# Rows and constants on GpSimd's queue, first weights issued by ScalarE, other banks for one projection, units dealt out anew

## The chip, the cores and the metric

The kernel runs on one core of one Trainium2 chip. TensorE (PE) multiplies, PEld is its loading of weights; VectorE (DVE), ScalarE (ACT) and GpSimd (POOL) work on tiles in the on-chip memory, and SyncE (SP) here only issues transfers. Each engine runs its own instructions in a fixed order and waits on semaphores for the others. The metric is the time of the whole program on the device in microseconds, as a median of several executions.

## The reference

One decoder layer for 256 tokens of width 2048, in fp32: a combined projection, two kinds of attention, their gated merge, an MLP with squared ReLU, and a gated embedding.

```python
h = rmsnorm(x, g_mix)
proj = h @ w_in                                  # 2048 -> 10240
qa, ka, va, qb, kb, vb, ga, gb = jnp.split(proj, splits, axis=-1)
ya = dilated_mixture(qa, ka, va)                 # three windowed patterns, 8 heads
yb = stick_breaking(qb, kb, vb)                  # 8 heads
merged = sigmoid(ga) * (ya @ w_branch_a) + sigmoid(gb) * (yb @ w_branch_b)
x = x + merged @ w_out
x = x + jnp.square(jax.nn.relu(rmsnorm(x, g_mlp) @ w_up)) @ w_down   # D_FF = 8192
x = x + (p @ w_ple_proj) * sigmoid(rmsnorm(x, g_ple) @ w_ple_gate)
```

## The kernel before

Every fp32 operand is split into two parts of a faster format: ScalarE copies it to a rounded high part (`wh` for weights, L82; with a gain for `h`, L85), and VectorE subtracts that from the original to get the low part (`wl`, L83; L86). A product is then three matmuls, high·high, high·low and low·high (L137 to L139 in the projections). Weights come in tiles of 1 MB by `load` on SP's queue (L91) into `raw`; `raw`, `wh` and `wl` have three buffers each, so a transfer, a split and a matmul of different tiles overlap and each waits for the buffer that it takes.

**Start.** The first projection runs in groups of 512 output columns; a group takes four chunks of weights, four 128-row pieces of the 2048 each. The first group has a function of its own, `first_weights(c)` for c = 0 to 3: it loads the columns of transposed x (`load_x`, L183) and the chunk of weights (L192 in three parts for c = 0, L91 after it), splits four pieces of `h` out of `x0` or `x1`, and splits the weights. With c = 3 it also calls `load_rows` (L229), which brings x by rows as `xr0` and `xr1`, 1 MB each, and loads the identity `idt`, the constants `cs` and the gains `gq` (L201 to L203). `xr0` and `xr1` lie in the pool of `x0` and `x1` and take over their buffers, so these loads wait until `x0` and `x1` have been read. ScalarE squares the rows (L232) for the norm `rt` (L212 to L219), which scales the projection's results (L250).

**MLP.** The hidden width is done in eight stages of 1024. `up_units(s)` makes a stage's 16 half units: per 128 hidden columns 16 pairs of matmuls, one of 512 columns (L526) and one of 256 (L527), then `ev` and the sum `hs` (L533), and `hidden` (L502 to L511) with ScalarE's square, four subtractions `hr` and the split into `u`. The way down has two halves of 1024 output columns per stage. In stages 0 to 6 the first half is done by `fast_units`: seven products in place of eight (L546, L548, L550, banks of the tag "s"), with sums of the weights' quarters `quart` on VectorE (L560, 128x2048) between them and sums of the products into the rows `xr` (L560 also, and `add_rows`, L446 and L448). The second half is done by `plain_units`, eight units (L628 to L630, two banks of the tag "m").

**The order.** `together` deals the units of three streams by due times: unit i of n of a stream with offset `first` is due at (i + first) / n. `up_units(s + 1)` runs in the same stage as the ways down of s. The program text that this makes is then ordered by a scheduler for each engine, and small works are put off by `later` until a modelled clock has advanced. The lines of the changed kernel are two less than those of before, from `first_weights` on.

Of the kernel before, what the change touches and what calls it, by code (L numbers as in the profile page):

```python
# [9 lines left out]
F32 = mybir.dt.float32  # L10
# [6 lines left out]
P = 128  # L17
# [5 lines left out]
DH = 128  # L23
# [6 lines left out]
C_ID, C_ONES, C_TRI, C_LOGC, C_SBM, C_COS, C_SIN = 0, 128, 256, 384, 768, 1152, 1184  # L30
# [29 lines left out]
def layer_kernel(ctx: ExitStack, tc: tile.TileContext, xt, xm, pt, gains, qkg, cst,  # L60
                 wa, wba, wbb, wo, wup, wdn, wpg, wpp, out):
    nc = tc.nc
# [26 lines left out]
    def load(src, nk, cols):  # L89
        raw = wts.tile([P, nk, cols], F32, tag="raw", name="raw")  # L90
        nc.sync.dma_start(raw.rearrange("p k c -> p (k c)"), src)  # L91
        return raw
# [89 lines left out]
    def load_x(a, b):  # L182
        nc.sync.dma_start(x[a // 8][:, a % 8:(b - 1) % 8 + 1, :], xt[:, a:b, :])  # L183

    def first_weights(c):

        k = 4 * c
        if c == 0:
            raw = wts.tile([P, 4, 512], F32, tag="raw", name="raw")
            for a, b in ((0, 1), (1, 2), (2, 4)):  # L190
                load_x(a, b)
                nc.sync.dma_start(raw[:, a:b, :].rearrange("p k c -> p (k c)"),  # L192
                                  wa[0, 0, :, a * 512:b * 512])
        else:
            load_x(k, k + 4)
            raw = load(wa[0, c], 4, 512)
        for i in range(k, k + 4):
            split(h[i][:, 0, :], h[i][:, 1, :], xs(i), gn[:, 0, i:i + 1])
        if c == 3:
            load_rows()  # L200
            nc.sync.dma_start(idt, cst[:, C_ID:C_ID + P])  # L201
            nc.sync.dma_start(cs, cst)
            nc.sync.dma_start(gq, bass.AP(tensor=qkg.tensor, offset=qkg.offset,  # L203
                                          ap=[[0, P], [DH, 2], [1, DH]]))
        return split_weights(raw, 4, 512, 1 if c == 0 else 2)

    def rows_norm(ss, name, pool):
# [17 lines left out]
    def load_rows():  # L225

        xr.extend(block([P, D], F32, f"xr{tt}", blk) for tt in range(2))
        for tt in range(2):
            nc.sync.dma_start(xr[tt], xm[tt])  # L229

    def squares_rows(tt, g, ss, junk):
        nc.scalar.activation(junk, xr[tt][:, g * PIECE:(g + 1) * PIECE], AF.Square,  # L232
# [259 lines left out]
    def bank2(tag, bufs=1):  # L492
        return ps2.tile([P, 512], F32, tag=tag, name=f"ps_{tag}", bufs=bufs)
# [21 lines left out]

    A21, A11, A22, A12, S3, S1, S2, S4 = range(8)

    def up_units(s, out, tag="mm"):

        for g in range(4):  # L520
            sums = mw.tile([P, 2, T], F32, tag="hs", name="hs", bufs=2)
            for j in range(2):
                ps = bank2(tag, 4 if tag == "s" else 2)
                parts = split_weights(load(wup[4 * s + g, j], DT, P), DT, P)
                for kt, (wh, wl) in enumerate(parts):
                    nc.tensor.matmul(ps, wh, flat(h2[kt]), start=kt == 0, stop=False)  # L526
                    nc.tensor.matmul(ps[:, :T], wl, h2[kt][:, 0, :], start=False, stop=kt == DT - 1)  # L527
                    advance(0.347)
                    if kt == 7:
                        yield  # L530
                t = mw.tile([P, T], F32, tag="ev", name="ev", bufs=2)
                nc.scalar.activation(t, ps[:, T:], AF.Copy)
                nc.vector.tensor_tensor(sums[:, j, :], ps[:, :T], t, op=ALU.add)  # L533
                if j == 1:
                    out.append(hidden(sums, (s, 0) in FAST or (s, 1) in FAST))
                yield
# [81 lines left out]
    def plain_units(s, n, u):  # L618

        for j in range(2):  # L620
            ps = [bank2("s", 4) if j and s == 7 else bank2("m", 2) for _ in range(2)]
            for i in range(2):
                raw = load(wdn[s, n, i, j], 4, PIECE)
                for k, (wh, wl) in enumerate(split_weights(raw, 4, PIECE)):
                    for tt in range(2):
                        a = 2 * i + tt
                        last = i == 1 and k == 3
                        nc.tensor.matmul(ps[tt], u[k][:, 0, a, :], wh, start=i + k == 0, stop=False)  # L628
                        nc.tensor.matmul(ps[tt], u[k][:, 0, a, :], wl, start=False, stop=False)  # L629
                        nc.tensor.matmul(ps[tt], u[k][:, 1, a, :], wh, start=False, stop=last)  # L630
                    advance(1.36)
                    if k == 1:
                        yield
                if i == 0:
                    yield
            for tt in range(2):
                add_rows(tt, (2 * n + j) * PIECE, ps[tt], r2[:, tt:tt + 1])
            yield
# [52 lines left out]
            finished(2 * n + 1)  # L691

    hids = [[]]
    for _ in up_units(0, hids[0], "s"):
        pass
    for s in range(7):
        hids.append([])
        streams = [(0.5, 16, up_units(s + 1, hids[s + 1]))]
        for n in range(2):
            if (s, n) in FAST:  # L700
                streams.append((0.3, 7, fast_units(s, n, hids[s])))
            else:
                streams.append((0.75, 8, plain_units(s, n, hids[s])))
        together(*streams)
    together((0.5, 16, last_units(hids[7])), (0.25, 4, embedding_units()))
    later(6, lambda: rms.append(rows_norm(ss2, "rt2", mw)))
# [88 lines left out]
```

## Time and profile before

| what | value |
|---|---|
| median of 3 runs | 1492.02 us (1491.55 to 1495.32) |
| profiled execution, own time | 1492.93 us |
| profiled execution, span of the trace | 1491.10 us |
| mean granted clock of TensorE | 0.997 of full |
| TensorE busy | 1470.8 us, 99% |
| VectorE busy | 1000.4 us, 67% |
| ScalarE busy | 840.3 us, 56% |
| GpSimd busy | 42.4 us, 3% |

All times of the trace are from one execution. Its own time is what the runs measure too; the span is the part that the trace covers, from its first instruction to its last. Matmuls overlap in the trace, so their spacing from start to start tells their cost, and the time printed for one does not.

### The profile page before, as it was taken

Reading aid. Unit: us, or ns where it says so; the run is one execution under the profiler, and the core shown is the slowest. Engines: PE = TensorE matmul, PEld = TensorE weight load, DVE = VectorE, ACT = ScalarE, POOL = GpSimd, SP = SyncE. Lnnn points to the kernel's source line nnn. Section 1 sums busy time; section 2 is a strip of 40 time slices with the busy share of each in tenths; the row PEclk is TensorE's granted clock in tenths of the full one; section 3 lists DMA queues with packets and bytes.
Section 4 is the critical chain, followed back from the end, with each engine's and each line's share of the span. In section 5 each row is a group of like instructions: output and inputs, shape, how many; then the busy total and the mean of one; then the engine's idle time right before and its main releaser. Section 6 shows DMA issues by size and latency. Waiting matters only on the chain.

```text
span 1491.1 us, 17831 instructions
## 1 busy us (share of the span) xinstructions
PE 1470.8 (99%) x6960; PEld 1210.2 (81%) x6960; DVE 1000.4 (67%) x1209; ACT 840.3 (56%) x1084; POOL 42.4 (3%) x60
## 2 busy tenths in 40 slices
PE   7999999999999999999999999999999999999998
PEld 5888888888888888888787887878888787878886
DVE  5775555456555555556878879788787878765654
ACT  7444555488834444546655656656565655656543
POOL 0442000000000000000000000000000000000000
PEclk9999999999999999999999999999999999999999
DMA  8555544544455555557455464645546465444563
GB/s 330 174 196 193 175 155 159 194 169 170 169 182 190 193 185 186 194 178 302 141 198 198 170 226 140 228 170 191 204 155 239 143 208 191 159 146 154 201 221 111
DMA packets 40549, 279.09 MB, mean 187 GB/s; under 512 B 4624, under 2 KB 5136, under 8 KB 7312
## 3 DMA queue, kind: packets, MB, share of 16 engines
q1 hardware_dynamic: 40320, 277.92, 53.5%
q8 instruction: 54, 0.88, 0.2%
q14 instruction: 31, 0.25, 0.0%
q10 hardware_dynamic: 144, 0.02, 0.0%
HBM read 275.83 MB, written 2.10 MB: 186 GB/s over the span
## 4 chain that ended last, share of the span: by engine, by line
PE 92%; DVE 3%; issue 2%; DMA 1%; ACT 1%; SPq 0%; DVEq 0%; ACTq 0%
PE ps_mm L137 13%; PE ps_mm L139 13%; PE ps_mm L526 13%; PE ps_mm L138 13%; PE ps_mm L527 7%; PE ps_m L629 4%; PE ps_m L630 4%; PE ps_m L628 3%; PE ps_s L548 3%; PE ps_s L546 2%; PE ps_s L550 2%; PE ps_s L526 2%; DVE wl L83 2%; DMA raw<-in_wa 1%; ACT wh L82 1%
## 5 line engine op out<-in xcount | busy, mean ns | idle before, releaser
L83 DVE TENSOR_TENSOR wl<-raw,wh 128x1024 fp32r<-128x1024 f32 (+1 forms) x462 | 563.5, 1228 | 341.3 <-ACT wh L82 337.8
L82 ACT ACTIVATE wh<-raw 128x1024 fp32r<-128x1024 f32 (+1 forms) x462 | 485.3, 1054 | 404.2 <-PE ps_mm L139 222.8
L526 PE MATMUL ps_mm<-h,wh 128*128 128x512 f32 x896 | 321.3, 398 | 0.0
L137 PE MATMUL ps_mm<-wh,h 128*128 128x512 f32 x640 | 255.8, 400 | 5.5 <-ACT wh L82 5.5
L527 PE MATMUL ps_mm<-h,wl 128*128 128x256 f32 x896 | 251.8, 281 | 0.4
L138 PE MATMUL ps_mm<-wl,h 128*128 128x512 f32 x640 | 251.2, 393 | 0.6 <-DVE wl L83 0.5
L139 PE MATMUL ps_mm<-wh,h 128*128 128x512 f32 x640 | 251.0, 392 | 0.0
L526 PEld LDWEIGHTS ps_mm<-h,wh 128*128 128x128 f32 x896 | 168.3, 188 | 40.8 <-ACT wh L82 2.3
L83 DVE TENSOR_TENSOR wl<-quart,wh 128x1024 fp32r<-128x1024 f32 x98 | 120.1, 1225 | 83.3 <-ACT wh L82 83.2
L527 PEld LDWEIGHTS ps_mm<-h,wl 128*128 128x128 f32 x896 | 169.0, 189 | 8.2 <-DVE wl L83 3.2
L82 ACT ACTIVATE wh<-quart 128x1024 fp32r<-128x1024 f32 x98 | 104.0, 1061 | 123.2 <-PE ps_mm L526 87.0
L137 PEld LDWEIGHTS ps_mm<-wh,h 128*128 128x128 f32 x640 | 121.0, 189 | 31.7 <-ACT wh L82 8.1
L138 PEld LDWEIGHTS ps_mm<-wl,h 128*128 128x128 f32 x640 | 121.3, 189 | 26.8 <-DVE wl L83 2.6
L139 PEld LDWEIGHTS ps_mm<-wh,h 128*128 128x128 f32 x640 | 121.0, 189 | 25.8
L629 PE MATMUL ps_m<-wl,u 128*128 128x512 f32 x256 | 101.8, 397 | 4.1 <-DVE wl L83 4.0
L630 PE MATMUL ps_m<-wh,u 128*128 128x512 f32 x256 | 100.0, 391 | 0.0
L628 PE MATMUL ps_m<-wh,u 128*128 128x512 f32 x256 | 97.9, 392 | 1.6 <-DVE xr L448 1.6
L548 PE MATMUL ps_s<-wl,u 128*128 128x512 f32 x196 | 80.2, 409 | 0.0
L546 PE MATMUL ps_s<-wh,u 128*128 128x512 f32 x196 | 78.6, 401 | 0.0
L550 PE MATMUL ps_s<-wh,u 128*128 128x512 f32 x196 | 76.7, 392 | 0.0
L560 DVE TENSOR_TENSOR quart<-quart 128x2048 f32<-128x2048 f32 x28 | 64.1, 2289 | 0.5
L629 PEld LDWEIGHTS ps_m<-wl,u 128*128 128x128 f32 x256 | 48.1, 188 | 18.1 <-DVE wl L83 9.2
(204 smaller groups left out, 1826.0 us busy)
## 6 DMA issues: line engine op xcount, KB each, us to landing
raw<-in_wa SPq DMA_DIRECT2D x79, 1024.0 KB, 4.8
raw<-in_wup SPq DMA_DIRECT2D x64, 1024.0 KB, 4.8
raw<-in_wdn SPq DMA_DIRECT2D x36, 1024.0 KB, 4.8
quart<-in_wdn SPq DMA_DIRECT2D x28, 1024.0 KB, 4.8
raw<-in_wo SPq DMA_DIRECT2D x16, 1024.0 KB, 4.8
raw<-in_wpg SPq DMA_DIRECT2D x16, 1024.0 KB, 4.8
raw<-in_wba SPq DMA_DIRECT2D x8, 1024.0 KB, 4.8
raw<-in_wbb SPq DMA_DIRECT2D x8, 1024.0 KB, 4.8
```

The costliest lines, as they stand in the source:

```text
L82: nc.scalar.activation(hi, src, AF.Copy)
L83: nc.vector.tensor_tensor(lo, src, hi.bitcast(F32), op=ALU.subtract)
L137: nc.tensor.matmul(ps[tt], lhs[kt][:, 0, t], wh, start=kt == 0, stop=False)
L138: nc.tensor.matmul(ps[tt], lhs[kt][:, 0, t], wl, start=False, stop=False)
L139: nc.tensor.matmul(ps[tt], lhs[kt][:, 1, t], wh, start=False, stop=kt == last)
L526: nc.tensor.matmul(ps, wh, flat(h2[kt]), start=kt == 0, stop=False)
L527: nc.tensor.matmul(ps[:, :T], wl, h2[kt][:, 0, :], start=False, stop=kt == DT - 1)
L546: nc.tensor.matmul(ps, f[k][:, 0, a, :], wh, start=start and k == 0, stop=False, skip_group_check=not start)
L548: nc.tensor.matmul(ps, f[k][:, 0, a, :], wl, start=False, stop=False, skip_group_check=not start)
L628: nc.tensor.matmul(ps[tt], u[k][:, 0, a, :], wh, start=i + k == 0, stop=False)
L629: nc.tensor.matmul(ps[tt], u[k][:, 0, a, :], wl, start=False, stop=False)
L630: nc.tensor.matmul(ps[tt], u[k][:, 1, a, :], wh, start=False, stop=last)
```

## The change

There are four edits. The rows of x and the three constants are issued by GpSimd, with `idt` ahead of the rows. The weights of the first group's chunks 0 and 1 are issued by ScalarE, those of chunks 2 and 3 by SP as before, and x comes by SP. The first up projection takes its banks from the tags "mm" and "m" in turn and no longer from "s". In `together` the fast units' offset goes from 0.3 to 0.6 and the plain units' from 0.75 to 0.3.

```diff
@@ -184,24 +184,22 @@
 
     def first_weights(c):
 
+
         k = 4 * c
-        if c == 0:
-            raw = wts.tile([P, 4, 512], F32, tag="raw", name="raw")
-            for a, b in ((0, 1), (1, 2), (2, 4)):
-                load_x(a, b)
-                nc.sync.dma_start(raw[:, a:b, :].rearrange("p k c -> p (k c)"),
-                                  wa[0, 0, :, a * 512:b * 512])
-        else:
-            load_x(k, k + 4)
-            raw = load(wa[0, c], 4, 512)
+        raw = wts.tile([P, 4, 512], F32, tag="raw", name="raw")
+        for a, b in ((0, 1), (1, 2), (2, 4)) if c == 0 else ((0, 4),):
+            load_x(k + a, k + b)
+            queue = nc.scalar if c < 2 else nc.sync
+            queue.dma_start(raw[:, a:b, :].rearrange("p k c -> p (k c)"),
+                            wa[0, c, :, a * 512:b * 512])
         for i in range(k, k + 4):
             split(h[i][:, 0, :], h[i][:, 1, :], xs(i), gn[:, 0, i:i + 1])
         if c == 3:
+            nc.gpsimd.dma_start(idt, cst[:, C_ID:C_ID + P])
             load_rows()
-            nc.sync.dma_start(idt, cst[:, C_ID:C_ID + P])
-            nc.sync.dma_start(cs, cst)
-            nc.sync.dma_start(gq, bass.AP(tensor=qkg.tensor, offset=qkg.offset,
-                                          ap=[[0, P], [DH, 2], [1, DH]]))
+            nc.gpsimd.dma_start(cs, cst)
+            nc.gpsimd.dma_start(gq, bass.AP(tensor=qkg.tensor, offset=qkg.offset,
+                                            ap=[[0, P], [DH, 2], [1, DH]]))
         return split_weights(raw, 4, 512, 1 if c == 0 else 2)
 
     def rows_norm(ss, name, pool):
@@ -226,7 +224,7 @@
 
         xr.extend(block([P, D], F32, f"xr{tt}", blk) for tt in range(2))
         for tt in range(2):
-            nc.sync.dma_start(xr[tt], xm[tt])
+            nc.gpsimd.dma_start(xr[tt], xm[tt])
 
     def squares_rows(tt, g, ss, junk):
         nc.scalar.activation(junk, xr[tt][:, g * PIECE:(g + 1) * PIECE], AF.Square,
@@ -515,12 +513,12 @@
 
     A21, A11, A22, A12, S3, S1, S2, S4 = range(8)
 
-    def up_units(s, out, tag="mm"):
+    def up_units(s, out, tags=("mm", "mm")):
 
         for g in range(4):
             sums = mw.tile([P, 2, T], F32, tag="hs", name="hs", bufs=2)
             for j in range(2):
-                ps = bank2(tag, 4 if tag == "s" else 2)
+                ps = bank2(tags[j], 2)
                 parts = split_weights(load(wup[4 * s + g, j], DT, P), DT, P)
                 for kt, (wh, wl) in enumerate(parts):
                     nc.tensor.matmul(ps, wh, flat(h2[kt]), start=kt == 0, stop=False)
@@ -691,16 +689,16 @@
             finished(2 * n + 1)
 
     hids = [[]]
-    for _ in up_units(0, hids[0], "s"):
+    for _ in up_units(0, hids[0], ("mm", "m")):
         pass
     for s in range(7):
         hids.append([])
         streams = [(0.5, 16, up_units(s + 1, hids[s + 1]))]
         for n in range(2):
             if (s, n) in FAST:
-                streams.append((0.3, 7, fast_units(s, n, hids[s])))
+                streams.append((0.6, 7, fast_units(s, n, hids[s])))
             else:
-                streams.append((0.75, 8, plain_units(s, n, hids[s])))
+                streams.append((0.3, 8, plain_units(s, n, hids[s])))
         together(*streams)
     together((0.5, 16, last_units(hids[7])), (0.25, 4, embedding_units()))
     later(6, lambda: rms.append(rows_norm(ss2, "rt2", mw)))
```

SP's queue behind the first group's last weights (`raw_237`), before. `raw_366` are the first weights of group 2:

```order
L91 DMA raw_237<-in_wa 128x2048
L229 DMA xr0_247<-in_xm 128x2048
L229 DMA xr1_248<-in_xm 128x2048
L201 DMA idt_84<-in_cst 128x128
L202 DMA cs_83<-in_cst 128x1216
L203 DMA gq_85<-in_qkg 128x256
L91 DMA raw_366<-in_wa 128x2048
```

And the whole start of SP's queue in the changed kernel, in which `raw_236` are the first group's last weights:

```order
L183 DMA x0_73<-in_xt 128x256 x2
L183 DMA x0_73<-in_xt 128x512
L183 DMA x0_73<-in_xt 128x1024
L193 DMA raw_193<-in_wa 128x2048
L183 DMA x1_74<-in_xt 128x1024 x2
L193 DMA raw_236<-in_wa 128x2048
L91 DMA raw_366<-in_wa 128x2048
```

The five transfers between the two have left SP's queue, and so have chunks 0 and 1 of the weights. GpSimd's queue in the changed kernel begins with these:

```order
L198 DMA idt_84<-in_cst 128x128
L200 DMA cs_83<-in_cst 128x1216
L201 DMA gq_85<-in_qkg 128x256
L227 DMA xr0_248<-in_xm 128x2048
L227 DMA xr1_249<-in_xm 128x2048
```

They are the only transfers of GpSimd, ahead of its other work. ScalarE's instructions at the start, before (`gn` are the gains, `raw_95` is chunk 0, `raw_151` chunk 1):

```order
L85 ACTIVATE h0_86<-x0_73,gn_75 128x256
L82 ACTIVATE wh_110<-raw_95 128x512
L85 ACTIVATE h0_86<-x0_73,gn_75 128x256
L82 ACTIVATE wh_114<-raw_95 128x512
L85 ACTIVATE h0_86<-x0_73,gn_75 128x256 x2
L82 ACTIVATE wh_118<-raw_95 128x512
L82 ACTIVATE wh_122<-raw_95 128x512
L85 ACTIVATE h1_87<-x0_73,gn_75 128x256 x4
L82 ACTIVATE wh_161<-raw_151 128x1024
```

And in the changed kernel, where chunk 1 is `raw_150`:

```order
L157 DMA gn_75<-in_gains 128x48
L193 DMA raw_95<-in_wa 128x512 x2
L193 DMA raw_95<-in_wa 128x1024
L85 ACT_TABLE_LOAD
L85 ACTIVATE h0_86<-x0_73,gn_75 128x256 x4
L82 ACTIVATE wh_110<-raw_95 128x512
L82 ACTIVATE wh_114<-raw_95 128x512
L82 ACTIVATE wh_118<-raw_95 128x512
L193 DMA raw_150<-in_wa 128x2048
L82 ACTIVATE wh_122<-raw_95 128x512
L85 ACTIVATE h1_87<-x0_73,gn_75 128x256 x4
L82 ACTIVATE wh_161<-raw_150 128x1024
```

The four splits of `h0` moved ahead of the first weights, and the issue of chunk 1 stands behind `wh_118`.

VectorE in a steady stage of the MLP, before. Names on `quart` are quarters of the fast units' weights, `raw` weights of the up projection or the plain units:

```order
L83 TENSOR_TENSOR wl_7035<-raw_7032,wh_7034 128x1024
L83 TENSOR_TENSOR wl_7039<-raw_7032,wh_7038 128x1024
L83 TENSOR_TENSOR u_6934<-hr_6928,u_6934 128x1024
L533 TENSOR_TENSOR hs_6951<-ps_mm_6952,ev_7027 128x256
L560 TENSOR_TENSOR quart_6981<-quart_6981,quart_6983 128x2048
L83 TENSOR_TENSOR wl_7058<-raw_7055,wh_7057 128x1024
L83 TENSOR_TENSOR wl_7062<-raw_7055,wh_7061 128x1024
L560 TENSOR_TENSOR xr1_248<-xr1_248,cp_7008 128x512
L83 TENSOR_TENSOR wl_7083<-quart_6979,wh_7082 128x1024
L83 TENSOR_TENSOR wl_7093<-quart_6979,wh_7092 128x1024
L560 TENSOR_TENSOR quart_6979<-quart_6979,quart_6983 128x2048
L83 TENSOR_TENSOR wl_7151<-raw_7148,wh_7150 128x1024
```

And at a like place in the changed kernel; `wl_7786` and `wl_7790` are up weights, `wl_7852` and `wl_7862` weights of a fast product, `wl_7878` the next up weights:

```order
L83 TENSOR_TENSOR wl_7751<-quart_7731,wh_7750 128x1024
L531 TENSOR_TENSOR hs_7679<-ps_mm_7680,ev_7779 128x256
L558 TENSOR_TENSOR quart_7731<-quart_7731,quart_7733 128x2048
L83 TENSOR_TENSOR wl_7786<-raw_7783,wh_7785 128x1024
L83 TENSOR_TENSOR wl_7790<-raw_7783,wh_7789 128x1024
L83 TENSOR_TENSOR wl_7852<-quart_7731,wh_7851 128x1024
L558 TENSOR_TENSOR quart_7733<-quart_7733,quart_7735 128x2048
L83 TENSOR_TENSOR wl_7862<-quart_7731,wh_7861 128x1024
L558 TENSOR_TENSOR xr1_249<-xr1_249,cp_7760 128x512
L558 TENSOR_TENSOR quart_7731<-quart_7731,quart_7735 128x2048
L531 TENSOR_TENSOR hs_7679<-ps_mm_7782,ev_7837 128x256
L83 TENSOR_TENSOR wl_7878<-raw_7875,wh_7877 128x1024
```

In the first piece two sums of `quart` stand among the eleven instructions ahead of the last; in the second there are three. TensorE, in the changed kernel, comes to `wl_7878` thus:

```order
L548 MATMUL ps_s_7850<-wh_7861,u_7491 128x512
L544 MATMUL ps_s_7850<-wh_7861,u_7676 128x512
L546 MATMUL ps_s_7850<-wl_7862,u_7676 128x512
L548 MATMUL ps_s_7850<-wh_7861,u_7676 128x512
L524 MATMUL ps_mm_7874<-h2_0_4384,wh_7877 128x512
L626 MATMUL ps_m_7707<-wh_7904,u_7119 128x512
L525 MATMUL ps_mm_7874<-h2_0_4384,wl_7878 128x256
```

Its matmuls on `wl_7862` end there and the next half unit of the up projection begins.

## Rows read from the trace of the kernel before

**Rows 1.** The page's first part: busy us of each engine, share, instructions.
```profile
PE 1470.8 (99%) x6960; PEld 1210.2 (81%) x6960; DVE 1000.4 (67%) x1209; ACT 840.3 (56%) x1084; POOL 42.4 (3%) x60
```

**Rows 2.** Waits of TensorE by line: us in total, times, longest.
```profile
PE ps_mm L137 <- ACT wh L82: 5.5, 3, 3.6
PE ps_m L629 <- DVE wl L83: 4.0, 7, 1.2
...
PE ps_s L526 <- DVE xr L446: 1.0, 1, 1.0
```

**Rows 3.** Timeline of TensorE, 31 to 42 us: start, duration, operation.
```profile
30.83 0.39 PE L138 MATMUL ps_mm<-wl,h 128*128 128x512 f32 x1
...
31.74 0.39 PE L139 MATMUL ps_mm<-wh,h 128*128 128x512 f32 x1
35.68 1.22 PE L137 MATMUL ps_mm<-wh,h 128*128 128x512 f32 x2 [3.56 <-ACT wh L82]
...
41.80 0.40 PE L138 MATMUL ps_mm<-wl,h 128*128 128x512 f32 x1
```

**Rows 4.** Windows: busy us and instructions of each engine, PEclk, DMA share, GB/s.
```profile
35.00:40.00 5.00, 4.28 (x9) 2.98 (x10) 4.46 (x10) 3.33 (x5) 0.00 (x0) 0.50 0.69 252
895.00:984.00 89.00, 88.46 (x438) 72.24 (x437) 72.46 (x83) 52.41 (x63) 0.00 (x0) 1.00 0.55 189
```

**Rows 5.** The chain of waits, its two transfers of the start: start, duration.
```profile
4.01 9.46 DMA raw<-in_wa
...
24.42 10.13 DMA raw<-in_wa
```

**Rows 6.** Timeline of ScalarE, start of the program.
```profile
9.32 1.15 ACT L82 ACTIVATE wh<-raw 128x512 fp32r<-128x512 f32 x2 [0.72 <-DMA raw<-in_wa]
...
13.57 2.00 ACT L82 ACTIVATE wh<-raw 128x1024 fp32r<-128x1024 f32 x2 [0.85 <-DMA raw<-in_wa]
...
34.57 2.00 ACT L82 ACTIVATE wh<-raw 128x1024 fp32r<-128x1024 f32 x2 [0.77 <-DMA raw<-in_wa]
```

**Rows 7.** Timeline of SyncE's queue, 13 to 24 us.
```profile
13.27 9.56 SPq L229 DMA_DIRECT2D xr<-in_xm  x2
22.88 0.44 SPq L201 DMA_DIRECT2D idt<-in_cst  x1
```

**Rows 8.** The page's transfers: KB each, us from issue to landing.
```profile
raw<-in_wa SPq DMA_DIRECT2D x79, 1024.0 KB, 4.8
```

**Rows 9.** Timeline of TensorE, first matmul of chunk 1.
```profile
14.68 0.74 PE L137 MATMUL ps_mm<-wh,h 128*128 128x512 f32 x2 [1.37 <-ACT wh L82]
```

**Rows 10.** Timeline of TensorE, first plain product of the last stage.
```profile
1339.97 0.47 PE L628 MATMUL ps_m<-wh,u 128*128 128x512 f32 x1 [1.56 <-DVE xr L448]
```

**Rows 11.** Timeline of VectorE in the steady stage.
```profile
905.09 0.42 DVE L533 TENSOR_TENSOR hs<-ps_mm,ev 128x256 f32<-128x256 f32 x1
905.42 2.28 DVE L560 TENSOR_TENSOR quart<-quart 128x2048 f32<-128x2048 f32 x1
907.62 2.35 DVE L83 TENSOR_TENSOR wl<-raw,wh 128x1024 fp32r<-128x1024 f32 x2
909.89 0.69 DVE L560 TENSOR_TENSOR xr<-xr,cp 128x512 f32<-128x512 f32 x1
910.49 1.22 DVE L83 TENSOR_TENSOR wl<-quart,wh 128x1024 fp32r<-128x1024 f32 x1
```

**Rows 12.** Timeline of TensorE in the steady stage.
```profile
898.74 0.28 PE L527 MATMUL ps_mm<-h,wl 128*128 128x256 f32 x1
...
899.32 0.40 PE L550 MATMUL ps_s<-wh,u 128*128 128x512 f32 x1
...
900.94 0.39 PE L526 MATMUL ps_mm<-h,wh 128*128 128x512 f32 x1
...
901.64 0.62 PE L628 MATMUL ps_m<-wh,u 128*128 128x512 f32 x2
902.72 0.50 PE L629 MATMUL ps_m<-wl,u 128*128 128x512 f32 x1 [0.47 <-DVE wl L83]
```


## Prediction

> **What bounds the kernel now.** I read the page's list of busy time first: TensorE is busy for 1470.8 us of the span, ScalarE and VectorE far less [rows 1]. So only time in which TensorE stands still or runs at the lower clock can be won, and none of the four edits takes a matmul away. Next came TensorE's waits by line: the largest is the first projection's, 5.5 us in three waits of which one has 3.6; then the plain products' second matmul, seven waits for VectorE with 4.0 in all, and 1.0 at the first up projection [rows 2].
>
> The timeline around the longest wait shows what it costs. In the first group matmuls start 0.228 us apart (30.83 to 31.74, four steps); the next one is due at 31.97 and starts at 35.68, 3.71 late. After the gap the granted clock is 0.50, half of TensorE's full 2.4 GHz [rows 4], and the 13 matmuls from 35.68 to 41.80 take 6.12 where 13 times 0.228 is 2.96: another 3.16 lost [rows 3]. Together 6.9 us. The chain of waits tells why: the weights of group 2 are issued at 24.42 and land 10.13 later; ScalarE's split of them at 34.57 waited for that transfer [rows 5, 6]. They were issued so late because SP's queue stood from 13.27 for 9.56 us at the two rows of x (their buffers are those of `x0` and `x1`, still being read) and went through three constants next [rows 7].
>
> In the MLP a stage takes 89 us, TensorE is busy for 88.46 of it, VectorE for 72.46 [rows 4]. VectorE has 16 us to spare on average, but its order is fixed, so a piece in which it has more work than TensorE between two needs shows as a wait.
>
> **The change part by part, the start.** With the rows and constants on GpSimd's queue, SP's order has group 2's weights directly behind the first group's last ones. Nothing else stands before them but the buffer they take, so the 6.9 us go. GpSimd itself does nothing until far behind that, so its waits for `x0` and `x1` hold nobody; the first readers of the rows on ScalarE (squares) stand early in its order too, but only in front of weights needed later, and cost nothing as long as the rows land by about 29. What the removed constants pay is their transfer: 64+608+128 KB, now among the first loads.
>
> The price is in the first group. ScalarE now issues the weights of chunks 0 and 1, and its order does all four splits of `h0` before the first weights, with chunk 1's issue only behind the split `wh_118`. Before, SP issued chunk 1 at 4.01, and it landed at 13.57 [rows 5, 6]. Now: the chunk that `wh_118` splits was there at 9.32 [rows 6]. It is later by the constants' transfer: below by nothing, above by 3.8 us (0.8 of the 4.8 us that 1 MB of these weights takes to land at the median [rows 8]); most of it overlaps, I take 1.5. One split (two take 1.15 [rows 6]) and an issue (0.44 for one of SP's [rows 7]) add 1.0, so the issue ends at 11.8. The landing takes 4.8 at the median [rows 8] and 9.46 in the crowded start [rows 5]; most of the crowd has been moved by then, so I take 6.0. From landing to matmul it was 1.11 (13.57 to 14.68 [rows 6, 9]). So chunk 1 starts at 9.32+1.5+1.0+6.0+1.1 = 18.9 instead of 14.68: 4.2 lost. Bounds: 9.32+0+1.0+4.8+1.1 = 16.2, 1.5 lost; 9.32+3.8+1.0+9.46+1.1 = 24.7, 10 lost. The later start of the very first matmuls lies inside this. **Start: 6.9 − 4.2 = −2.7 us**, between −5.4 and +3.1.
>
> The row shows SP's queue standing still for 9.56 us [rows 7], not working. The Trainium skill, page "DMA: Bandwidth & Descriptors", section "Issuing engines are not separate DMA queues", says that transfers run on the same 16 DMA engines whoever starts them, and that several issuers save only the initiation time, usually small. By it alone this part would give back 1.5 us (the three issues from 22.88 to 24.42) and the start would lose 2.7; by the row the saving is the standing time, and I go by the row.
>
> **First up projection.** It gets the four banks of the tags "mm" and "m" in place of those of "s". Its wait is 1.0 us [rows 2], for VectorE's sum of the rows. The order shows the same matmul behind the same sum before and now: **0**, bounded by −1.0 if the wait goes, and by +1.0 if the banks are freed as late again.
>
> **Units dealt out anew, the end of the MLP.** Plain units come earlier against the fast ones. At 1339.97 the last stage's first plain product waits 1.56 for the `add_rows` by which VectorE frees a bank of stage 6 [rows 10]. Now stage 6's plain units come ahead of its last fast units, and VectorE's order has that `add_rows` ahead of theirs: **−1.6**, bounded by 0 if a new wait stands there.
>
> **Units dealt out anew, the seven stages.** Two of VectorE's sums `quart`, 128x2048, were spread between weights; now three stand within eleven instructions, as VectorE's rows in the change show. I price that piece by spacings [rows 11]: sum 2.20 (905.42 to 907.62), weights 1.13 each (two from 907.62 to 909.89), `hs` 0.33 (905.09 to 905.42), a row sum 0.60 (909.89 to 910.49). From behind `wl_7751` to the end of `wl_7878`: three sums, two `hs`, four weights, one row sum, and `wl_7878` itself with 1.2: 6.60+0.66+4.52+0.60+1.2 = 13.6 us. Meanwhile TensorE has, from the first need of `wl_7751` to the first of `wl_7878`, 42 matmuls of 512 columns and 16 of 256. A pair of both takes 0.348 (four pairs and one of 0.228 from 899.32 to 900.94 [rows 12]): 16 pairs are 5.57, the other 26 at 0.228 are 5.93, 11.5 in all. VectorE falls behind by 2.1, if it comes to `wl_7751` just in time. It does nearly: the buffer of the weights is freed about 2.5 us ahead of the need, and split and subtraction take that long. Some 0.2 more follow at `wl_7905`.
>
> From it goes what the stage of before loses in the same way: from 901.64 two matmuls take 1.08 where 0.46 is due, 0.62 (of which 0.47 is the wait) [rows 12]; 0.11 behind it; and a late piece of 0.23 (898.74 to 899.32 takes 0.58, where 0.348 is due [rows 12]), which stands three times in a stage: 0.7. The new order has wider gaps at all of these. Per stage: +2.1+0.2−0.6−0.1−0.7 = +0.9, in seven stages **+6.3 us**. Bounds: if VectorE comes to `wl_7751` 2 us early, the lateness is gone and only the gains stay, 7 × −1.4, of which I count half (−5), since the gaps move elsewhere; if nothing of the old loss goes, 7 × 2.3 = 16; half the gains gone, +12.
>
> **Sum.** The profiled execution took 1492.93 (span 1491.10 and 1.83 around it), 0.9 above the median of 1492.02. 1492.93 − 2.7 + 0 − 1.6 + 6.3 = 1494.9, less 0.9: **1494**.
>
> **The rivals.** 0.3% is 4.5 us, about what a measurement of this kernel can tell from no change: same is 1487.5 to 1496.5.
>
> (1) *Faster:* VectorE reaches the dense piece ahead and absorbs it; it has 16 us to spare in a stage [rows 4], and wherever TensorE stalls elsewhere it gets further ahead. Against it: it also waits for ScalarE's split and that for the buffer, so it can't run far ahead. Then the MLP costs between 0 and −5: 1492.9−2.7−1.6 = 1488.6 down to 1483.6, less 0.9: 1483 to 1488, with the middle at 1485. Chance 0.27, since the lateness rests on one window of 2.5 us.
>
> (2) *Slower, the start gains nothing:* chunk 1 is a serial chain (x, four splits, weights, split, issue, landing). If TensorE runs out of chunk 0 more than some 3 us before it, as in the gap before, the granted clock falls again and costs another 3.2 [rows 3, 4]: start +0.5, the time 1497. With a landing of 9.46 as well, 3.5 more: 1501. It decides from chunk 1 at about 19 on. For it: TensorE has only 24 matmuls to do until then. Against it: a wait in the first group as short as 1.37 [rows 9] cost no clock. A third way to the same place is that only the three constants' issues come back (1.5 from 22.88 to 24.42 [rows 5, 7]) and the two rows' standing time returns as a later landing: 1.5 − 4.2 = +2.7 for the start, 1499. Chance of the three 0.17, of this one 0.04 in it, since group 2's weights took only 10.13 behind a late issue [rows 5]. That one is what the skill's rule on issuing engines would make of it.
>
> (3) *Slower, a second dense piece:* if VectorE is late at another weight in each stage too, by half of the first (1.0), 7 us more: 1499 to 1505. For it: the sums must stand somewhere, and the plain products, whose waits are VectorE's already [rows 2], now come at other points. Chance 0.10.
>
> That the orders don't change is excluded by the rows of the change.
>
> **How the numbers follow.** My forecast, 1494, has 0.46, with a range of its own from 1488 to 1498. Case 1 ends under 1487.5 for nearly all of its 0.27. Cases 2 and 3 lie above 1496.5 and hold 0.27 together. So faster 0.27, same 0.46, slower 0.27. For 8 in 10 I leave the lowest tenth of case 1 and the upper half of case 3 with the end of case 2 out: 1484 to 1501.
>
> **What would show it.** In the profile after: no wait of 3.6 on the first projection's first matmul behind the first group, and 1.00 of the clock from 30 to 45; chunk 1's first matmul between 16 and 20; SP's queue without a row of x; the 1.56 at the last stage gone; and in each stage one wait of about 2 at the first up matmul that takes a new `wl` from `raw` behind the three sums. The prediction is wrong if that wait is absent (rival 1), if the clock falls within the first 25 us (rival 2), or if waits stand at two weights per stage (rival 3).

## The result, and the profile after

The changed kernel takes 1504.75 us (median of 4 runs, 1503.77 to 1504.98), the kernel before in the same comparison 1492.26. The ratio is 1.0078, with a 95% interval from 1.0061 to 1.0096: slower, by about 12 us. The profiled execution took 1503.77 with a span of 1501.6, 10.8 and 10.5 more than that of before.

TensorE's waits by line (us in total, times, longest), to be read beside [rows 2]:

```profile
PE ps_m L626 <- ACT wh L82: 10.5, 7, 1.5
PE ps_mm L137 <- ACT wh L82: 8.3, 2, 6.1
PE ps_mm L525 <- DVE wl L83: 3.5, 7, 1.1
...
PE ps_mm L524 <- DVE xr L444: 1.0, 1, 1.0
```

The wait at the plain products has another releaser: no longer VectorE's `wl`, but ScalarE's `wh`, with 1.5 in each of seven stages. VectorE's seven waits now stand at the up products. The first projection has 8.3 where it had 5.5. The first up projection's 1.0 is where it was.

TensorE's timeline: the first group and the beginning of the second, the first matmul of the MLP, and the last stage's first plain product:

```profile
11.30 1.22 PE L137 MATMUL ps_mm<-wh,h 128*128 128x512 f32 x2 [6.06 <-ACT wh L82]
...
22.19 0.73 PE L137 MATMUL ps_mm<-wh,h 128*128 128x512 f32 x2 [2.26 <-ACT wh L82]
...
24.64 0.63 PE L137 MATMUL ps_mm<-wh,h 128*128 128x512 f32 x1
...
27.20 0.62 PE L137 MATMUL ps_mm<-wh,h 128*128 128x512 f32 x1
...
40.84 0.39 PE L139 MATMUL ps_mm<-wh,h 128*128 128x512 f32 x1
41.07 0.39 PE L137 MATMUL ps_mm<-wh,h 128*128 128x512 f32 x1
...
672.20 0.47 PE L524 MATMUL ps_mm<-h,wh 128*128 128x512 f32 x1 [0.98 <-DVE xr L444]
...
1350.12 0.39 PE L626 MATMUL ps_m<-wh,u 128*128 128x512 f32 x1
```

And the window in which its matmuls slow down (busy us and instructions of PE, PEld, DVE, ACT, POOL; granted clock; DMA share; GB/s):

```profile
24.60:27.60 3.00, 3.00 (x8) 2.31 (x7) 2.65 (x5) 1.59 (x4) 0.00 (x0) 0.50 0.76 246
```

The first matmul on weights starts at 11.30 (4.94 in the kernel before); in the row of 22.19 chunk 1 begins, 7.5 us later than the 14.68 of [rows 9]. From 24.64 to 27.20 six matmuls take 2.56, 0.43 each, where 0.228 is the pace at the full clock; the granted clock in this window is 0.50. But the first group's last matmul, at 40.84, is followed by group 2's first at 41.07: the gap of [rows 3] is gone.

So, counted by matmuls of the same number, the changed kernel is 9.1 us behind at the end of the first group and 2.2 from group 2 on. At the first matmul of the MLP it is still 2.2 behind (672.20 against 669.98). When the last stage's first plain product is due, it is 11.9 behind (1350.12 against 1338.25, a step behind the matmul at 1338.02), and a few matmuls later 10.3, as the bank wait of [rows 10] is gone. The sum of it: +2.2 at the start, +9.7 in the stages, −1.5 at the end.

### The profile page after: what moved, and what is told of

It reads as the page before. It is cut to its first block, busy times and chain, and to the rows that moved or that the text cites. A ratio compares the mean times of both kernels' runs of the same rounds, so it can differ in the third digit from the quotient of the medians.

```text
span 1501.6 us, 17725 instructions
## 1 busy us (share of the span) xinstructions
PE 1470.5 (98%) x6960; PEld 1210.5 (81%) x6960; DVE 1003.9 (67%) x1209; ACT 843.7 (56%) x1085; POOL 47.4 (3%) x65
## 4 chain that ended last, share of the span: by engine, by line
PE 94%; DVE 2%; issue 1%; DMA 1%; ACT 1%; ACTq 0%; DVEq 0%
PE ps_mm L524 15%; PE ps_mm L139 13%; PE ps_mm L138 13%; PE ps_mm L137 13%; PE ps_mm L525 8%; PE ps_m L626 4%; PE ps_m L627 4%; PE ps_m L628 3%; PE ps_s L544 3%; PE ps_s L546 3%; PE ps_s L548 3%; DMA raw<-in_wa 1%; ACT wh L82 1%; PE ps_m L524 1%; PE ps_s L725 1%
## 5 line engine op out<-in xcount | busy, mean ns | idle before, releaser
L524 PE MATMUL ps_mm<-h,wh 128*128 128x512 f32 x960 | 345.9, 396 | 1.0 <-DVE xr L444 1.0
L525 PE MATMUL ps_mm<-h,wl 128*128 128x256 f32 x960 | 271.8, 283 | 3.5 <-DVE wl L83 3.5
L137 PE MATMUL ps_mm<-wh,h 128*128 128x512 f32 x640 | 255.8, 400 | 8.3 <-ACT wh L82 8.3
L524 PEld LDWEIGHTS ps_mm<-h,wh 128*128 128x128 f32 x960 | 180.3, 188 | 43.0 <-issue 1.4
L525 PEld LDWEIGHTS ps_mm<-h,wl 128*128 128x128 f32 x960 | 181.0, 189 | 16.1 <-DVE wl L83 12.2
L137 PEld LDWEIGHTS ps_mm<-wh,h 128*128 128x128 f32 x640 | 121.1, 190 | 34.1 <-ACT wh L82 10.3
L626 PE MATMUL ps_m<-wh,u 128*128 128x512 f32 x256 | 99.2, 396 | 10.5 <-ACT wh L82 10.5
L626 PEld LDWEIGHTS ps_m<-wh,u 128*128 128x128 f32 x256 | 47.0, 188 | 22.8 <-ACT wh L82 13.4
```

What stands on the lines that cost most here:

```text
L137: nc.tensor.matmul(ps[tt], lhs[kt][:, 0, t], wh, start=kt == 0, stop=False)
```

## The first group's lateness

ScalarE's timeline and queue in the changed kernel (ACTq are issues):

```profile
10.64 1.14 ACT L82 ACTIVATE wh<-raw 128x512 fp32r<-128x512 f32 x2
14.48 0.63 ACT L82 ACTIVATE wh<-raw 128x512 fp32r<-128x512 f32 x1 [2.71 <-DMA raw<-in_wa]
14.49 0.33 ACTq L193 DMA_DIRECT2D raw<-in_wa  x1
...
21.08 2.01 ACT L82 ACTIVATE wh<-raw 128x1024 fp32r<-128x1024 f32 x2 [3.84 <-DMA raw<-in_wa]
```

SP's queue in the same kernel:

```profile
3.13 0.33 SPq L193 DMA_DIRECT2D raw<-in_wa  x1
4.62 1.11 SPq L183 DMA_DIRECT2D x<-in_xt  x2
16.47 0.33 SPq L193 DMA_DIRECT2D raw<-in_wa  x1
24.55 34.45 SPq L91 DMA_DIRECT2D raw<-in_wa  x7
```

And the two transfers in its chain of waits (start, duration):

```profile
2.14 12.31 DMA raw<-in_wa
...
14.49 6.49 DMA raw<-in_wa
```

Chunk 0's last half, issued at 2.14, landed 12.31 us later, and its split starts at 14.48 where it was 9.32 [rows 6]. Only behind the start of this split stands chunk 1's issue, at 14.49; it landed 6.49 later, and 22.19 follows. Why chunk 0 took 12.31: SP's queue, with little to wait for, had issued chunk 2's megabyte at 3.13 and the last megabyte of x at 4.62, while GpSimd had issued 0.8 MB of constants. On one queue, chunk 0 had stood ahead of all these. Now three queues send side by side. Their traffic from 4 to 10 us (packets, MB, share of the 16 engines; by the bytes that each moves in all, q1 is SP's, q0 GpSimd's and q10 ScalarE's):

```profile
q1 hardware_dynamic: 257, 0.72, 34.0%
q0 software_dynamic: 170, 0.68, 31.8%
q10 hardware_dynamic: 251, 0.65, 31.4%
```

In the kernel before, SP's queue was alone in the same window:

```profile
q1 hardware_dynamic: 609, 1.86, 90.5%
```

The Trainium skill, page "DMA: Bandwidth & Descriptors", section "Issuing engines are not separate DMA queues", says that transfers of several issuers run on the same 16 engines and interleave; this trace agrees, with about a third for each queue and 12.31 us for 512 KB.

Four kernels take the start apart. The first has the rows and constants on GpSimd's queue and nothing else (two of its five loads are shown).

```diff
-            nc.sync.dma_start(xr[tt], xm[tt])
+            nc.gpsimd.dma_start(xr[tt], xm[tt])
...
-            nc.sync.dma_start(cs, cst)
+            nc.gpsimd.dma_start(cs, cst)
```

> Only the rows of x and the three constants are moved to GpSimd's queue. Theory: the first group was late in the changed kernel because its weights and x were shared out over three queues whose transfers run side by side, where one queue gave them in the order of need; the constants' 0.8 MB alone delay the first group by 1 to 3 us, while the 6.9 us before group 2 go: 4 to 6 us faster, 1486 to 1488. Rival: the constants among the first loads are what cost the 9.1 us of the first group; then this kernel is 2 us slower than before or the same.

Measured: 1489.22, ratio 0.9976 (0.9967 to 0.9985). Chunk 0's last half is split at 11.44, 2.1 later than before; the first group is 1.8 late and the gap mostly gone; behind group 2 it is 3.3 us ahead. The constants alone are not what cost the first group 9.1; the gain is 1 to 3 us short of the 4 to 6.

The second has only the weights of chunks 0 and 1 issued by ScalarE.

```diff
+            queue = nc.scalar if c < 2 else nc.sync
+            queue.dma_start(raw[:, a:b, :].rearrange("p k c -> p (k c)"),
+                            wa[0, c, :, a * 512:b * 512])
```

> Only the first weights are issued by ScalarE (chunks 0 and 1). Theory: the first group is 7 to 9 us later than before, the gap before group 2 partly hidden behind that; net 2 to 9 us slower, 1494 to 1501. Rival (the constants alone cost it): the first group is less than 3 us later.

Measured: 1493.13, ratio 1.0003 (0.9994 to 1.0013): the same. The first group ends 7.6 late, so ScalarE's issuing costs most of it by itself; and 6.9 come back at the gap, though SP still issues the rows. The expected loss was too high by 1 us or more: the gap hides behind a late first group. ScalarE's timeline in this kernel:

```profile
10.85 0.63 ACT L82 ACTIVATE wh<-raw 128x512 fp32r<-128x512 f32 x1 [0.80 <-DMA raw<-in_wa]
10.86 0.33 ACTq L192 DMA_DIRECT2D raw<-in_wa  x1
```

SP sends the constants here and GpSimd nothing, so two queues share the engines, ScalarE's with 41.1% from 4 to 10 us. Chunk 0's last half landed 8.69 us after its issue, and its split is 1.5 late instead of 5.2.

The third has only the two rows on GpSimd's queue.

> Only the two rows of x go to GpSimd's queue; the constants stay on SP's, behind the first group's last weights. Theory: SP's queue no longer stands still, group 2's weights are issued about 8 us earlier, the gap of 3.7 and the 3.2 at the lower clock both go, and nothing is added at the start: 6 to 7 us faster, 1485 to 1486. Rival (the landing, not the issue, held group 2's weights): less than 3 us faster.

Measured: 1492.81, ratio 1.0005 (0.9995 to 1.0014). Nothing is won, the theory fell. SP's queue in this kernel:

```profile
16.30 33.23 SPq L91 DMA_DIRECT2D raw<-in_wa  x6
```

TensorE's waits (us in total, times, longest):

```profile
PE ps_mm L137 <- ACT wh L82: 6.8, 3, 4.9
```

The second row's transfer in the chain of waits:

```profile
22.02 10.68 DMA xr<-in_xm
```

And ScalarE's timeline:

```profile
32.72 0.63 ACT L232 ACTIVATE junk<-xr 128x512 f32<-128x512 f32 x1 [4.96 <-DMA xr<-in_xm]
...
35.18 1.04 ACT L82 ACTIVATE wh<-raw 128x1024 fp32r<-128x1024 f32 x1
```

Group 2's weights are issued from 16.30 on, 8 us earlier. But TensorE's longest wait at L137 is now 4.9, since ScalarE stood 4.96 at the squares of the second row (`xr`) and comes to the split of group 2's weights, which stands behind them in its order, at 35.18. That row was issued at 22.02, hardly earlier than before (its buffer had still to be read), and landed 10.68 us later, beside group 2's weights; in the kernel before its squares began at 27.53. So part of the time that the queue stood came back as a later landing of the row. In the kernel before, both conditions ended almost together: ScalarE was through with what stands ahead of the split at 33.8, and the transfer ended at 34.6 [rows 5, 6]. The last of that work on ScalarE, in the kernel before:

```profile
33.12 0.69 ACT L250 ACTIVATE qraw<-ps_mm,rt 128x512 f32<-128x512 f32 x1 [1.11 <-DVE rt L219]
```

In the changed kernel the gap is gone mainly because the first group ends after both.

The fourth is the whole change, but with chunk 1 on SP (`c < 1` in place of `c < 2`).

> The whole change, but chunk 1 of the first weights is issued by SP and only chunk 0 by ScalarE. In the changed kernel the first group ends 9.1 us later than before. Theory: it is late by the serial chain through ScalarE (chunk 0's last part landed at 14.5 instead of 9.3, only then chunk 1 was issued, at 14.49, and landed 6.5 later). With chunk 1 on SP behind x, chunk 1 follows x in order of need: the first group ends 3 to 6 us late, TensorE's wait of 2.3 for chunk 1 and the lower clock after it go. The total then gains little (0 to 2 us against the changed kernel, 1503 to 1505), since the rows' squares hold group 2 until about 35 in any case. Rival: the traffic of all queues together, not the chain, makes chunk 1 late; then the first group stays 8 to 10 us late.

Measured: 1501.59 (ratio to before 1.006, 1.0042 to 1.0079), 3.2 less than the changed kernel. The first group ends 2.7 late instead of 9.1: 6.4 us of the lateness are chunk 1's place behind ScalarE's split, and it gives back a little more than was expected. Chunk 0's last half is split at 12.75 here, although SP had issued a megabyte more by then, so the bytes that the other queues hold do not by themselves set its lateness; why it is 1.7 earlier than in the changed kernel was not followed.

To see the gap go without any of the price, the rows and constants were issued on SP's queue behind three chunks of group 2's weights, with the norm's work behind group 2 in the program.

```diff
+    def second_weights(c):
+        raw = load(wa[1, c], 4, 512)
+        if c == 2:
             load_rows()
...
+                ps = group_m(range(4), h, second_weights)
                 rt = x_norm()
```

> The kernel before, with the rows of x and the constants issued behind the first three chunks of group 2's weights, still on SP's queue, and the norm's work behind group 2 in the program. ScalarE's order then has the splits of group 2's weights ahead of the squares of the rows. Theory: the gap before group 2 has two causes that end together, the late issue of its weights and the squares that wait for the second row ahead of its split on ScalarE; with the row moves alone the second one kept the gap (4.9 us, from 32 to 36). With both gone, 6 to 7 us faster than before: 1485 to 1486. Rival: the results of the first group then wait for the norm and group 3 finds no bank: 2 to 4 of it come back.

Measured: 1487.93, ratio 0.9972 (0.9961 to 0.9983): faster than both kernels, by 4.7 and by 16.8 us. SP's queue in it:

```profile
26.40 1.32 SPq L233 DMA_DIRECT2D xr<-in_xm  x2
```

And TensorE's waits:

```profile
PE ps_m L640 <- DVE wl L83: 4.0, 7, 1.2
...
PE ps_mm L137 <- ACT wh L82: 1.4, 2, 1.0
```

The rows are issued from 26.40 on and hold SP's queue for 1.32 us, and the wait at L137 falls to 1.4 in all. Behind group 2 it is 7.2 us ahead, as the theory has it; 2.0 of that are lost again by matmul 400, as much as the rival says but not for a bank (waits of 0.3 and 0.5 for VectorE are among them).

## The stages

TensorE's timeline at one of the seven places, in the changed kernel:

```profile
823.58 0.39 PE L525 MATMUL ps_mm<-h,wl 128*128 128x256 f32 x1 [0.41 <-DVE wl L83]
...
831.77 0.39 PE L524 MATMUL ps_mm<-h,wh 128*128 128x512 f32 x1
833.66 0.50 PE L626 MATMUL ps_m<-wh,u 128*128 128x512 f32 x1 [1.50 <-ACT wh L82]
833.99 0.28 PE L525 MATMUL ps_mm<-h,wl 128*128 128x256 f32 x1
```

ScalarE's at the same place:

```profile
830.60 1.07 ACT L82 ACTIVATE wh<-raw 128x1024 fp32r<-128x1024 f32 x1 [0.18 <-PE ps_s L548]
831.97 0.69 ACT L554 ACTIVATE cp<-ps_s,r 128x512 f32<-128x512 f32 x1 [0.30 <-PE ps_s L548]
832.56 1.05 ACT L82 ACTIVATE wh<-raw 128x1024 fp32r<-128x1024 f32 x1
```

And VectorE's:

```profile
829.65 2.29 DVE L558 TENSOR_TENSOR quart<-quart 128x2048 f32<-128x2048 f32 x1
831.86 0.42 DVE L531 TENSOR_TENSOR hs<-ps_mm,ev 128x256 f32<-128x256 f32 x1
832.19 2.35 DVE L83 TENSOR_TENSOR wl<-raw,wh 128x1024 fp32r<-128x1024 f32 x2
```

TensorE does one up matmul at 831.77 and comes at 832.00 to L626, a plain unit's first matmul, which stands second there in its order (it is in the rows of the change). Its weights are split on ScalarE from 832.56, behind the copy `cp` of the product that has just ended, and TensorE stands 1.50. VectorE begins the first `wl` of the up weights at 832.19, behind the third sum; TensorE needs it at 832.00, so without L626 it would have stood until about 833.3 for VectorE. The two end within 0.3 us of each other, so the trace alone doesn't say which one to remove.

The offsets alone came first, the other edits undone.

```diff
-                streams.append((0.3, 7, fast_units(s, n, hids[s])))
+                streams.append((0.6, 7, fast_units(s, n, hids[s])))
...
-                streams.append((0.75, 8, plain_units(s, n, hids[s])))
+                streams.append((0.3, 8, plain_units(s, n, hids[s])))
```

> Only the offsets of the units (0.6 and 0.3) are changed. Theory: of the 10.8 us that the changed kernel's profiled execution is longer, 2.4 come from the start and the rest from the MLP's stages: about 1.5 lost in each of the seven, 2.3 won back at the last stage. So this kernel is 8 us slower than before (1500), with one wait of 1.5 per stage at a plain unit's first matmul for ScalarE. Rival: the waits in the stages come from the first up projection's banks or from the start's shift of the stages; then this one is within 2 us of before.

Measured: 1501.92, ratio 1.0058 (1.0043 to 1.0073), with the same seven waits of 1.5. By the ratio the offsets cost 8.7 us (6.4 to 10.9 by its interval); the changed kernel's trace has 9.7 in the stages less 1.5 at the end for them, and 2.2 for the start.

Then the fourth of the sums was taken out. It is the one of `quart` between the two other ones in VectorE's rows of the change (b01 plus b11), and it is not needed before the sixth product. The kernel without it leaves out that sum, so its sixth product multiplies other numbers.

```diff
-        sum_later(b[0, 1], b[1, 1])
```

> The two offsets alone, and the last of the four sums of the weights' quarters (quarter 01 plus quarter 11) is left out, so the products that need it compute something else. It stood early in VectorE's order, inside the dense piece, though its result is needed late. Theory: VectorE's lateness at the up weights behind the three sums is the cause of both waits there (1.5 for ScalarE's split at a plain unit's matmul, placed there because of that lateness, and 0.4 for VectorE): both go, 10 to 14 us faster than with the offsets alone (1501.9): 1488 to 1492. Rival: the plain unit's split, which waits for a buffer and a copy of a product on ScalarE, costs by itself: the wait of 1.5 stays, 1498 to 1502.

Measured: 1493.93, ratio 1.001 (1.0001 to 1.002), 7 to 8 us less than with the offsets alone. TensorE's waits:

```profile
PE ps_mm L527 <- DVE wl L83: 5.5, 14, 1.1
PE ps_mm L137 <- ACT wh L82: 5.0, 3, 3.2
```

No wait for ScalarE's `wh` is left at the plain products: with VectorE in time, TensorE's order has all eight pairs on the first split of the up weights ahead of the plain unit. Fourteen short waits for VectorE stay, 5.5 in all, and the time is 2 us above the forecast's 1492.

Is it the 2.2 us of work, or its place? The same sum was done in full, but held back until the fourth product's result is there.

```diff
         w0 = keep(pw, 0)
+        one = b[0, 1][:, 0, 0:1]
+        nc.vector.scalar_tensor_tensor(one, w0[:, 0:1], 0.0, one, op0=ALU.mult, op1=ALU.add)
         sum_later(b[0, 1], b[1, 1])
```

> The two offsets alone; the fourth sum is done in full on VectorE, but held back: a one-column operation on its first operand reads a result of the fourth product first. VectorE's order then has the sum behind the dense piece. Theory: the place of the sum in VectorE's order makes the loss, not its 2.2 us as such; so this runs like the kernel without the sum (1493.9): 1491 to 1496. Rival: the amount of VectorE's work per stage makes it; then it stays at 1499 to 1502.

Measured: 1493.97, ratio 1.0 (0.9991 to 1.0009). VectorE's timeline, the third sum, the holding operation and the fourth sum:

```profile
841.67 2.29 DVE L560 TENSOR_TENSOR quart<-quart 128x2048 f32<-128x2048 f32 x1
...
853.17 0.16 DVE L600 SCALAR_TENSOR_TENSOR quart<-cp,quart 128x1 f32<-128x1 f32 x1
...
854.25 2.29 DVE L560 TENSOR_TENSOR quart<-quart 128x2048 f32<-128x2048 f32 x1
```

The sum now stands at 854.25, 12.6 us behind the third, and the time is that of the kernel without it. So the place it is. In both kernels TensorE's order changed along with VectorE's: the plain unit's first matmul moved from between the pairs to behind them. The runs show that the sum's place makes the loss, through the orders that the scheduler makes of it; they do not show how much of it belongs to each of the two waits at that place.

GpSimd is idle there, and it was given the sum:

```diff
-        sum_later(b[0, 1], b[1, 1])
+        nc.gpsimd.tensor_tensor(b[0, 1], b[0, 1], b[1, 1], op=ALU.add)
```

> The two offsets alone, and the same fourth sum is done by GpSimd, which is idle in the MLP; nothing is left out. VectorE's order is that of the kernel without this sum. Theory: as there, 1488 to 1492, if GpSimd's sum (about 7 us by its 128x512 operations of 1.6 to 2.2) disturbs nobody. Rival: GpSimd's access slows VectorE's work beside it, or its result comes late for the sixth product: 1495 to 1502.

Measured: 1520.16, ratio 1.0183 (1.0168 to 1.0198), beyond the rival's range too. GpSimd's timeline in this kernel:

```profile
823.18 5.45 POOL L599 TENSOR_TENSOR quart<-quart 128x2048 f32<-128x2048 f32 x1 [87.87 <-DVE quart L560]
```

And VectorE's:

```profile
820.76 2.28 DVE L560 TENSOR_TENSOR quart<-quart 128x2048 f32<-128x2048 f32 x1
822.96 6.75 DVE L83 TENSOR_TENSOR wl<-raw,wh 128x1024 fp32r<-128x1024 f32 x2
```

While GpSimd adds for 5.45 us, two subtractions that take 2.35 elsewhere take 6.75.

Three more combine the parts. Held sum, old offsets, rows behind:

> The kernel with the rows behind group 2's weights (1487.9), old offsets, and the fourth sum held back in the same way. Theory: the waits of 4.0 at the plain products for VectorE come from the sums' places too, so up to 3 of it come back: 1485 to 1488. Rival: the old order has room for the fourth sum where it stands, and no time is won: 1487 to 1490.

Measured: 1495.14, ratio 1.0016 (1.0007 to 1.0025): neither. It is 7 us slower than without the hold. TensorE's waits:

```profile
PE ps_m L642 <- DVE wl L83: 4.2, 7, 1.2
PE ps_s L557 <- ACT wh L82: 3.8, 2, 2.2
```

The waits for VectorE at the plain products stayed, and new ones for ScalarE's `wh` at the fast products came, all of the loss in the first two stages. Why the late sum makes ScalarE late there was not followed. The rows behind and new offsets in the last stage alone:

> The kernel with the rows behind group 2's weights, and the new offsets in the last of the seven stages alone. Theory: the new offsets cost about 1.5 us in each stage and give back 2.3 at the bank wait of the last stage, so in the last alone they win 0.5 to 1.5: 1486 to 1487.5, faster than before by 0.35 to 0.4%. Rival: the last stage's wait comes back elsewhere: 1488 to 1490.

Measured: 1488.19, ratio 0.9966 (0.9954 to 0.9979), not told apart from 1487.93, so the win of 0.5 to 1.5 was not seen; the 1.5 of the changed kernel stands in this stage now. And rows behind, new offsets, held sum:

> The rows behind group 2's weights, the new offsets in all stages, and the fourth sum held back. Theory: the parts add: 1492 to 1494 less 4 to 6 from the start: 1487 to 1490. Rival: with the start's time won the stages' waits get longer: above 1492.

Measured: 1488.19, ratio 0.9967 (0.9955 to 0.9978): the parts add, but it is no faster than with the old order.

## Why the prediction was wrong

The forecast was 1494 and the range ended at 1501. Its two large terms were too good, and both in the same direction.

**The start** was put at −2.7 and measured +2.2. The 6.9 us of the gap went in full, though not for the reason given: with the rows moved alone the wait stayed, for ScalarE's order held the split. The squares of the rows were to cost nothing "as long as the rows land by about 29"; in that kernel the second row was there at 32.7. Rival 2's third way, a later landing of the rows, names this. The step that failed is the lateness of chunk 0's last part: "most of it overlaps, I take 1.5", with 3.8 as its bound, measured 5.2 (14.48 against 9.32). It counted the constants' transfer alone, which by the run with rows and constants moved makes 2.1. It left out that chunk 0 no longer stands ahead of chunk 2 and the rest of x on one queue: SP's queue, GpSimd's and its own share the engines, and its own got 31.4% of them. The rest of that sum nearly held: landing 6.49 (6.0 was taken) and 1.1 from there to the matmul; the 1.0 for a split and an issue did not appear, since the issue began 0.01 behind the split's start and its time lies in the 6.49. Chunk 1 so came at 22.19 instead of 18.9, past the point of 19 from which rival 2 had it decide; and as that rival said, the granted clock fell behind the wait, and cost about 1.6 us. The wait was 2.26 long, less than the some 3 that the rival asked for. Its +0.5 for the whole start was still 1.7 too low.

**The seven stages** were put at +6.3 and measured +9.7. The dense piece with three sums was the right place, as the sum's removal and its holding back show: 2.1 and 0.2 were forecast per stage, and the waits of 0.4 and 1.5 with the slow spacing around them come to 2.2. That the totals agree is in part luck. Behind the three sums 1.7 is lost (833.66, where 832.00 was due), and VectorE alone would have made it about 1.3; the other 0.6 stands at the up weights behind an earlier sum (823.58, where 823.02 was due), a second place such as rival 3 named, with 0.6 where it asked for 1.0. The releaser in the profile is another than the one named: TensorE's order, one row above `wl_7878`, has a plain unit's matmul whose split on ScalarE I hadn't priced, and it ends together with VectorE's. What was mis-sized is the part that goes from before: 1.4 per stage was taken off. Between the same waits of five steady stages it is 90.3 us a stage now (833.66 to 1285.01) and was 88.9 (813.94 to 1258.46), 1.4 more where 0.9 was forecast, so about 0.9 went and not 1.4; where the other 0.5 stands in the new order was not traced. Seven times 0.5 is about the 3.4 that are missing. One bound was also added up wrong: with half of the gains gone it is +11.2 and not +12.

**The first up projection** was put at 0, and its wait is 1.0 before and after. **The end** was put at −1.6 and gave −1.5.

**The sum**: 8.9 us lie between the forecast for the profiled execution, 1494.9, and the 1503.77 that it took, of which the start makes 4.9, the stages 3.4 and the end 0.1; 0.2 are lost behind the last matmul and 0.3 outside the span. The profiled execution was taken to be 0.9 above the median; it came 1.0 below, which is the rest. Rival 2 named its part of what happened, but in the sum over cases it stood alone, with the stages at their central value; the two losses together had been given no chance.

## What to carry to other kernels

A transfer queue that stands still also keeps order: when loads are spread over several issuers, what is needed last competes with what is needed first, so count every queue that is sending at the moment of need and not only the bytes that were moved. Before a wait is credited to the transfer that ended last, read the order of the engine behind it for a second condition that ends at the same time; here, the rows moved alone won nothing, and with both conditions removed TensorE was 7.2 us ahead behind group 2. And when a scheduler packs a piece of one engine, the price of a dense piece shows on whichever engine's work was placed into the hole: test it by moving one instruction out of the piece, keep its work, and look which other orders moved with it.

## What was not expected of the hardware

GpSimd's sum of two tiles of 128x2048 takes 5.45 us beside VectorE, and VectorE's two subtractions beside it 6.75 in place of 2.35; so 2.2 us taken off VectorE cost it 4.4. The Trainium skill, page "SBUF — State Buffer", section "Who interferes with whom", says that a VectorE instruction with two inputs in that memory contends with a GpSimd instruction that reads it; these two rows agree.
